# Gate maxima spread by a transfer, mLSTM products in float32r parts, first loads in small pieces, a shared last norm: one decoder layer

## The chip, the cores and the metric

The kernel runs on one core of a Trainium2 chip. The time is the device time of one execution in microseconds, as a median over runs. The engines are named as in the profile: PE is TensorE's matmul, PEld its weight load, DVE is VectorE, ACT ScalarE, POOL GpSimd, and SP the queue from which all transfers are issued. Each engine works through its own instructions in order and waits for the others by semaphores.

## The reference

One layer of a hybrid decoder, 256 tokens, model width 2048, all in float32. It has three steps, each followed by a layer norm over `alpha * x + f(x)`:

1. One input projection. Its columns go to eight attention heads of width 128 (a dilated window with a bias table), to four mLSTM heads of width 256, and to the mLSTM gates. Both groups' outputs go through one output projection.
2. Cross-attention, four heads of width 512, on 256 memory tokens.
3. A SwiGLU channel mixer, hidden width 5632.

The part that matters here is the mLSTM. With gate sums `b` and input gates `log_i`, a running maximum over time keeps the exponentials in range. Taken over all 256 tokens at once, a head is

```
u[r]      = log_i[r] - b[r],   mx[t] = max(0, u[0..t])
e[r,t]    = exp(u[r] - mx[t])  for r <= t, else 0
w[r,t]    = e[r,t] * (k[r] . q[t]) / sqrt(256)
num[t]    = sum_r w[r,t] * v[r],   den[t] = sum_r w[r,t]
h[t]      = num[t] / max(|den[t]|, exp(-(b[t] + mx[t])))
```

and `h` is normalised over its 256 columns and multiplied by the output gate. The last step of the layer is a layer norm `(z - mean) * scale * g + b` over 2048 columns, in four tiles of 512 for each half of the tokens.

## The kernel before

**Products in parts.** A float32 operand is split by `split` (L113 to L115) into a high part in float32r, by ScalarE's cast, and a low part, what is left, by VectorE's subtraction. A product is then three float32r matmuls: high by high, high by low, low by high. All large GEMMs are done so; many of them also by a seven-product scheme (`gemm_seven`). Products of operands left in plain F32 are single instructions in the program, and stand as two records each in the profile.

**Memory.** `big` gives one of 34 SBUF tiles of 128x1024 words, `slot` half of one, both reused first in, first out. PSUM has eight banks: five for GEMMs (`bank`), three for all else (`sbank`). Weights come by SP into three raw buffers of 1 MB (`RAW`), and are split into five pairs of parts (`SPLIT`).

**Order.** The program is written phase by phase: attention projections, bias table and attention, gates, mLSTM projections and heads, output projection, cross-attention, channel mixer, last norm. A planner that simulates the engines' times then orders the instructions of each engine; only one stretch (behind the second norm) has an order written by hand. So neighbouring phases overlap, and the order of all engines comes out of the planner's costs.

**Start.** A warm-up of `WARM = 2` F32 products of 512 columns on a zeroed tile (L429). Then the first projection `i0` (`gemm_features`, L387 and L388): eight steps of two k-tiles each; each step multiplies 1024 weight columns by the two tiles of x. `loader` (L181) brings x two k-tiles at a time; `weights` (L232) brings the weights, 1 MB for two steps, except the first: two halves of step 0 (L242) and step 1 by itself (L245).

**Gates.** `gates` (L510) computes `mx` as four rows (one for each head), and spreads row `h` over all 128 partitions by a product with a selecting matrix: `bc` (L551), plain F32 with four rows of contraction. VectorE forms `-mx + mask` from it (L553, L557), ScalarE the exponentials `e` (L559, L560). The selecting matrix `sel` is loaded at L794.

**mLSTM heads.** `mlstm` (L585) computes the scores (`ms`, L590), the weights `w` (L595), then for three blocks of w the products with the values (`mh`, 256 columns) and with a column of ones (`md`, one column), all in plain F32 (L603). Statistics (L608), the norm (L611 to L618), gate (L623) and transposes (L629) follow. Heads 0 and 1 stand in the program between the third value projection and `i6`, heads 2 and 3 before the keys `xk0` and `xk1`.

**End.** The last GEMM, `w2b1`, ends with the second half of the tokens; then `Norm.finish` (L719): mean and scale, four operations `(z - mean) * g` and four `z * scale + b`, all on VectorE (L726, L729), and one store for each tile (L1171).

## Time and profile before

| | us |
|---|---|
| runs | 1539.5, 1541.11, 1541.36 (median 1541.11) |
| the profiled execution's own time | 1540.81 |
| its span (first to last instruction or transfer) | 1539.0 |

| engine | busy us | share |
|---|---|---|
| PE | 1522.7 | 99% |
| DVE | 1233.4 | 80% |
| ACT | 797.0 | 52% |
| POOL | 9.3 | 1% |

The transfers move 301.37 MB, on average 196 GB/s; in the first of 40 equal slices of the span they move 303 GB/s, the most of any. The granted TensorE clock is full in all slices.

How to read the lines: a timeline line gives start and length in us, engine, line of the kernel, operation, the tiles written and read (buffer numbers left out), partitions x elements, and how many like it are merged; in brackets how long the engine sat idle before it, and what ended that. A line of waits gives who waited for whom, the sum in us, how often, and the longest. A slot keeps the name that its tile had when it was last made, so a name can be that of an earlier use.

### The profile page before, as it was taken

What the parts mean: (1) busy time and instruction counts of PE and PEld (TensorE: products, weight loads), DVE (VectorE), ACT (ScalarE), POOL (GpSimd) and SP (SyncE); (2) the same over time, 40 slices, a digit from 0 to 9 for tenths busy, and PEclk for the clock granted to TensorE, in tenths of its full rate; (3) what the DMA queues carried; (4) which work ended last, traced back from release to release, by engine and by line L of the source; (5) the groups of instructions that cost most, each with busy time, mean ns of one, the idle gap of its engine ahead of it and who ended that gap; (6) DMA issues with size and microseconds to landing.
All of it is one profiled execution on the core that took longest, in us unless ns stands there. A gap on an engine that the chain in (4) does not pass through costs nothing.

```text
span 1539.0 us, 19369 instructions
## 1 busy us (share of the span) xinstructions
PE 1522.7 (99%) x7394; PEld 1273.8 (83%) x7394; DVE 1233.4 (80%) x1663; ACT 797.0 (52%) x1054; POOL 9.3 (1%) x18
## 2 busy tenths in 40 slices
PE   9999999999999999999999999999999999999997
PEld 7888888888888878888888888887788888888885
DVE  7665788787799888657798788888788878888897
ACT  5444645554544555445557454555545455455551
POOL 0000000000000000000000000000000000000000
PEclk9999999999999999999999999999999999999999
DMA  8674445664654546445564555665455666567552
GB/s 303 208 272 165 140 172 210 232 237 160 232 191 172 205 171 221 162 165 179 177 218 165 174 182 192 218 195 200 156 215 208 200 192 194 192 205 260 197 186 109
DMA packets 83419, 301.37 MB, mean 196 GB/s; under 512 B 7213, under 2 KB 9466, under 8 KB 59774
## 3 DMA queue, kind: packets, MB, share of 16 engines
q1 hardware_dynamic: 83326, 300.14, 56.6%
q8 instruction: 58, 0.95, 0.2%
q14 instruction: 35, 0.29, 0.1%
HBM read 297.99 MB, written 4.21 MB: 196 GB/s over the span
## 4 chain that ended last, share of the span: by engine, by line
PE 95%; DVE 3%; DMA 1%; issue 0%; ACT 0%; DVEq 0%; SPq 0%; ACTq 0%
PE w2a1P L323 2%; PE w2a0P L323 2%; PE w2b0P L323 2%; PE w2b1P L323 2%; PE f10P L323 2%; PE v1P L323 2%; PE xo0P L323 2%; PE wo0P L323 2%; PE f4P L323 2%; PE f14P L323 2%; PE f6P L323 2%; PE f20P L323 2%; PE f16P L323 2%; PE f18P L323 2%; PE v0P L323 2%; PE wo1P L323 2%
## 5 line engine op out<-in xcount | busy, mean ns | idle before, releaser
L114 ACT CAST w2a1h<-w2a1w 128x1024 fp32r<-128x1024 f32 (+1 forms) x24 | 22.5, 980 | 23.3 <-PE w2a1E L323 14.5
L114 ACT CAST w2a0h<-w2a0w 128x1024 fp32r<-128x1024 f32 (+1 forms) x24 | 22.8, 980 | 17.8 <-PE w2a0E L323 10.7
L115 DVE TENSOR_TENSOR w2a0l<-w2a0w,w2a0h 128x1024 fp32r<-128x1024 f32 (+1 forms) x24 | 26.5, 1129 | 6.1 <-ACT w2a0h L114 6.1
L115 DVE TENSOR_TENSOR w2a1l<-w2a1w,w2a1h 128x1024 fp32r<-128x1024 f32 (+1 forms) x24 | 26.3, 1128 | 5.6 <-ACT w2a1h L114 5.6
L114 ACT CAST w2b0h<-w2b0w 128x1024 fp32r<-128x1024 f32 (+1 forms) x20 | 19.3, 987 | 17.3 <-PE w2b0E L323 9.8
L114 ACT CAST w2b1h<-w2b1w 128x512 fp32r<-128x512 f32 (+1 forms) x28 | 19.8, 758 | 12.9 <-PE w2b0E L323 5.4
L323 PE MATMUL w2a0P<-w2a0h,hT 128*128 128x512 f32 x80 | 26.2, 391 | 0.2 <-ACT w2a0h L114 0.2
L323 PE MATMUL w2a1P<-w2a1h,hT 128*128 128x512 f32 x80 | 25.4, 389 | 0.0
L114 ACT CAST wo1h<-wo1w 128x1024 fp32r<-128x1024 f32 (+1 forms) x16 | 15.6, 1001 | 18.9 <-PE wo1E L323 11.3
L264 PE MATMUL f0b<-f0h,x 128*128 128x512 f32 x64 | 25.4, 397 | 0.0
L114 ACT CAST f12h<-f12w 128x1024 fp32r<-128x1024 f32 (+1 forms) x16 | 15.6, 1000 | 18.7 <-PE f12E L323 9.9
L265 PE MATMUL f0b<-f0l,x 128*128 128x512 f32 x64 | 25.1, 392 | 0.1
L114 ACT CAST xv0h<-xv0w 128x1024 fp32r<-128x1024 f32 (+1 forms) x16 | 15.2, 970 | 18.5 <-PE xv0E L323 7.1
L115 DVE TENSOR_TENSOR w2b0l<-w2b0w,w2b0h 128x1024 fp32r<-128x1024 f32 (+1 forms) x20 | 22.2, 1137 | 3.0 <-ACT w2b0h L114 3.0
L115 DVE TENSOR_TENSOR v0l<-v0w,v0h 128x1024 fp32r<-128x1024 f32 (+1 forms) x16 | 18.2, 1154 | 7.8 <-ACT v0h L114 7.7
L115 DVE TENSOR_TENSOR xo0l<-xo0w,xo0h 128x1024 fp32r<-128x1024 f32 (+1 forms) x16 | 18.2, 1153 | 7.3 <-ACT xo0h L114 7.2
L114 ACT CAST v0h<-v0w 128x1024 fp32r<-128x1024 f32 (+1 forms) x16 | 15.7, 1000 | 16.0 <-PE v0E L323 9.9
L114 ACT CAST v2h<-v2w 128x1024 fp32r<-128x1024 f32 (+1 forms) x16 | 15.6, 1000 | 16.2 <-PE v2E L323 10.8
L115 DVE TENSOR_TENSOR w2b1l<-w2b1w,w2b1h 128x512 fp32r<-128x512 f32 (+1 forms) x28 | 22.7, 854 | 1.5 <-ACT w2b1h L114 1.5
L387 PE MATMUL i0b<-xT,i0h 128*128 128x512 f32 x64 | 22.6, 427 | 0.8 <-ACT i0h L114 0.8
L115 DVE TENSOR_TENSOR wo0l<-wo0w,wo0h 128x1024 fp32r<-128x1024 f32 (+1 forms) x16 | 18.2, 1153 | 6.4 <-ACT wo0h L114 6.4
L387 PE MATMUL xk1b<-mT,xk1h 128*128 128x512 f32 x64 | 23.0, 401 | 0.3 <-ACT xk1h L114 0.3
(1719 smaller groups left out, 5556.6 us busy)
## 6 DMA issues: line engine op xcount, KB each, us to landing
w2a0w<-in_w SPq DMA_DIRECT2D x12, 1024.0 KB, 4.8
w2a1w<-in_w SPq DMA_DIRECT2D x12, 1024.0 KB, 5.7
w2b0w<-in_w SPq DMA_DIRECT2D x10, 1024.0 KB, 4.9
w2b1w<-in_w SPq DMA_DIRECT2D x10, 1024.0 KB, 5.0
v0w<-in_w_v SPq DMA_DIRECT2D x8, 1024.0 KB, 5.1
v1w<-in_w_v SPq DMA_DIRECT2D x8, 1024.0 KB, 4.8
v2w<-in_w_v SPq DMA_DIRECT2D x8, 1024.0 KB, 4.8
wo0w<-in_w_out SPq DMA_DIRECT2D x8, 1024.0 KB, 4.9
```

Of the source, the lines that this page charges most:

```text
L114: SC.copy(hi, src)
L115: latest["lo"] = V.tensor_tensor(out=lo, in0=src, in1=as_f32(hi), op=ALU.subtract).ins
L264: T.matmul(banks[m][c], xh, wh[:, cs], start=n == 0, stop=False)
L265: T.matmul(banks[m][c], xh, wl[:, cs], start=False, stop=False)
L323: T.matmul(of[to], lhsT, rhs, start=to not in begun, stop=end)
L387: T.matmul(banks[f], wh[:, cs], op.both(kt), start=kt == 0, stop=end, skip_group_check=True)
```

## The change

Five edits:

- `WARM`: the second warm-up product has 256 columns in place of 512.
- `loader` and `weights`: for x and the first 1 MB of weights of `i0`, the loads are made in small pieces. x comes in single k-tiles (128 KB) for tiles 0 to 3; the weights of step 0 come in four pieces of 256 columns, those of step 1 in two of 512. Casts and subtractions follow the pieces. SP's order is: x 0, two weight pieces, x 1, two weight pieces, x 2, one weight piece, x 3, one weight piece.
- `gates`: the four rows of maxima are stored to DRAM and loaded back, repeated on all partitions, into one tile; `bc`'s products, `sel` and its load go.
- `mlstm`: the values and the weights are split into parts. The ones stand as two more columns beside the values' high part, so that the sum of the weights comes out of the same products: nine float32r products a head in place of six in F32. Each half of the tokens has its own PSUM bank, and the denominator is copied out by ScalarE.
- the last norm: for the second half of the tokens, tiles 0 and 1 are done as before, tiles 2 and 3 get `z * scale - mean * scale` from ScalarE and then a product with g and a sum with b on VectorE.

```diff
@@ -35,7 +35,7 @@
 W = 1024
 NSLOT, RAW, SPLIT = 34, 3, 5
 LAG, HEAD, POOLED, LAG2 = 6, 8, 5, 8
-WARM = 2
+WARM = (512, 256)
 
 SEVENS = (2, 4, 6, 8, 13, 15, 17)
 
@@ -178,8 +178,17 @@
         def both(self, kt):
             return self.parts[kt // 2][:, (kt % 2) * 512 : (kt % 2 + 1) * 512]
 
-    def loader(op, src):
+    def loader(op, src, fine=False):
+        def tile_alone(kt):
+            j, s = divmod(kt, 2)
+            raw = slot(f"{op.name}raw{kt}t")
+            nc.sync.dma_start(out=raw[:, :S], in_=src[j][:, s * S : (s + 1) * S])
+            hi, lo = op.views(j)
+            split(hi[:, s], lo[:, s], raw[:, :S])
+            free(raw)
 
         def load(j):
             if j not in op.parts:
@@ -188,6 +197,7 @@
                 op.put(j, raw)
                 free(raw)
 
+        load.tile_alone = tile_alone if fine else None
         return load
 
 
@@ -232,11 +242,19 @@
     def weights(src, n, name, load=None):
 
         for b in range(n // 2):
-            if load:
+            first = load is not None and b == 0
+            fine = first and load.tile_alone
+            if load and not fine:
                 load(b if n == KT else 2 * b)
-            first = load is not None and b == 0
             w = wp.tile([P, 2, W], F32, tag="w", name=f"{name}w{b}", bufs=RAW)
-            if first:
+            if fine:
+                for i in range(2):
+                    for s in range(2):
+                        load.tile_alone(2 * i + s)
+                        for c in range(2 - i):
+                            cs = slice(s * 512 + c * 256, s * 512 + (c + 1) * 256 * (1 + i))
+                            nc.sync.dma_start(out=w[:, i, cs], in_=src[b][:, i, cs])
+            elif first:
                 for c in range(2):
                     cs = slice(c * 512, (c + 1) * 512)
                     nc.sync.dma_start(out=w[:, 0, cs], in_=src[b][:, 0, cs])
@@ -251,8 +269,9 @@
                     load(at)
                 wh = wp.tile([P, W], F32R, tag="wh", name=f"{name}h{at}")
                 wl = wp.tile([P, W], F32R, tag="wl", name=f"{name}l{at}")
-                halves = (slice(0, 512), slice(512, 1024))
-                for cs in halves if first and i == 0 else (slice(0, 1024),):
+                n_cols = 256 * (1 + i) if fine else 512 if first and i == 0 else 1024
+                for c in range(0, 1024, n_cols):
+                    cs = slice(c, c + n_cols)
                     split(wh[:, cs], wl[:, cs], w[:, i, cs])
                 yield at, wh, wl
 
@@ -426,14 +445,14 @@
 
     idle, pw = slot("idle"), sbank("pw")
     G.memset(idle, 0.0)
-    for _ in range(WARM):
-        T.matmul(pw, idle[:, :P], idle, start=True, stop=True)
+    for n in WARM:
+        T.matmul(pw[:, :n], idle[:, :P], idle[:, :n], start=True, stop=True)
     free(idle)
     ones = const.tile([P, 1], F32, tag="ones", name="ones")
     V.memset(ones, 1.0)
 
     xT = Operand("xT")
-    load_x = loader(xT, A["xT"])
+    load_x = loader(xT, A["xT"], fine=True)
 
 
     def bias_table():
@@ -546,12 +565,15 @@
         V.tensor_copy(cols.rearrange("p a b -> p (a b)"), pc[:, :16])
 
         es = []
+        line = dram.tile([MH, S], F32, tag="mline", name="mline")
+        nc.sync.dma_start(out=line, in_=mx)
+        bcs = big("bcs", F32)
+        nc.sync.dma_start(out=bcs, in_=bass.AP(line.tensor, line.offset, [[0, P], [1, MH * S]]))
         for h in range(MH):
-            bc = sbank(f"bc{h}")
-            T.matmul(bc[:, :S], sel[:, h], mx, start=True, stop=True)
+            bc = bcs[:, h * S : (h + 1) * S]
             e = slot(f"me{h}")
             V.scalar_tensor_tensor(
-                out=e[:, :S].rearrange("p (m t) -> p m t", m=2), in0=bc[:, :S].rearrange("p (m t) -> p m t", m=2),
+                out=e[:, :S].rearrange("p (m t) -> p m t", m=2), in0=bc.rearrange("p (m t) -> p m t", m=2),
                 scalar=-1.0, in1=tri[:, None, :].to_broadcast([P, 2, P]), op0=ALU.mult, op1=ALU.add,
             )
             V.tensor_scalar(out=e[:, S : S + P], in0=bc[:, P:S], scalar1=-1.0, scalar2=None, op0=ALU.mult)
@@ -559,7 +581,7 @@
                 SC.activation(e[:, cs], e[:, cs], ACT.Exp, bias=cols[:, m, h : h + 1])
             SC.activation(e[:, S : S + P], e[:, S : S + P], ACT.Exp, bias=cols[:, 0, h : h + 1])
             es.append(e)
-        free(t0, t1, t2, t3, t4)
+        free(t0, t1, t2, t3, t4, bcs)
         return es, cols[:, 2:]
 
     def conv_silu(raw, ft, name):
@@ -595,19 +617,32 @@
         V.scalar_tensor_tensor(
             out=w[:, :384], in0=sc[:, :384], scalar=MD ** -0.5 / 4.0, in1=e[:, :384], op0=ALU.mult, op1=ALU.mult
         )
-        hb, dn = sbank(f"mh{h}"), sbank(f"md{h}")
-        vh = [v[r][h // 2][:, h % 2 * MD : (h % 2 + 1) * MD] for r in range(2)]
-        steps = ((0, 0, 0), (1, 0, S), (1, 1, P))
-        for n, (m, r, at) in enumerate(steps):
-            for o, x in ((hb[:, m * MD : (m + 1) * MD], vh[r]), (dn[:, m : m + 1], ones)):
-                T.matmul(o, w[:, at : at + P], x, start=n == 0, stop=n != 1, skip_group_check=True)
+        va, wa = big(f"mv{h}"), big(f"mwp{h}")
+        vh = [va[:, r * (MD + 2) : (r + 1) * (MD + 2)] for r in range(2)]
+        vl = [va[:, 2 * MD + 4 : 3 * MD + 4], wa[:, 768:]]
+        wh, wl = wa[:, :384], wa[:, 384:768]
+        for r in range(2):
+            split(vh[r][:, :MD], vl[r], v[r][h // 2][:, h % 2 * MD : (h % 2 + 1) * MD])
+            V.tensor_copy(vh[r][:, MD:], ones.to_broadcast([P, 2]))
+        split(wh, wl, w[:, :384])
+        hb = [sbank(f"mh{h}{m}") for m in range(2)]
+        for n, (m, r, at) in enumerate(((0, 0, 0), (1, 0, S), (1, 1, P))):
+            for a, x in ((wh, vh[r]), (wh, vl[r]), (wl, vh[r])):
+                cols = x.shape[-1]
+                T.matmul(
+                    hb[m][:, :cols], a[:, at : at + P], x, start=n != 2 and a is wh and cols > MD,
+                    stop=n != 1 and a is wl, skip_group_check=True,
+                )
+        free(va, wa)
         st = small.tile([P, 2, 6], F32, tag="mst", name=f"mst{h}")
         mv = small.tile([P, 2, 2], F32, tag="mmv", name=f"mmv{h}")
-        r = small.tile([P, 3, 2], F32, tag="mr", name=f"mr{h}")
+        r = small.tile([P, 4, 2], F32, tag="mr", name=f"mr{h}")
+        norm, rs, den = r[:, 0], r[:, 1], r[:, 3]
         for m in range(2):
-            V.bn_stats(out=st[:, m], in_=hb[:, m * MD : (m + 1) * MD])
+            SC.copy(den[:, m : m + 1], hb[m][:, MD : MD + 1])
+            V.bn_stats(out=st[:, m], in_=hb[m][:, :MD])
             V.bn_aggr(out=mv[:, m], in_=st[:, m])
-        den, norm, rs = dn[:, :2], r[:, 0], r[:, 1]
         V.scalar_tensor_tensor(
             out=norm, in0=den, scalar=-1.0, in1=least_norm[:, :, h], op0=ALU.mult, op1=ALU.max
         )
@@ -621,7 +656,7 @@
         for m in range(2):
             ym = y[:, m * MD : (m + 1) * MD]
             V.scalar_tensor_tensor(
-                out=ym, in0=hb[:, m * MD : (m + 1) * MD], scalar=mv[:, m, 0:1],
+                out=ym, in0=hb[m][:, :MD], scalar=mv[:, m, 0:1],
                 in1=gate[m][h // 2][:, h % 2 * MD : (h % 2 + 1) * MD], op0=ALU.subtract, op1=ALU.mult,
             )
             SC.activation(ym, ym, ACT.Copy, scale=r[:, 2, m : m + 1])
@@ -728,6 +763,21 @@
                 t = z[m][c]
                 V.scalar_tensor_tensor(out=t, in0=t, scalar=scale, in1=self.b[c], op0=ALU.mult, op1=ALU.add)
 
+        def finish_by_two(self, m):
+            mean, scale = self.scales(m)
+            shift = small.tile([P, 1], F32, tag="lsh", name=f"{self.name}sh{m}")
+            for t, g in zip(z[m][:2], self.g):
+                V.scalar_tensor_tensor(out=t, in0=t, scalar=mean, in1=g, op0=ALU.subtract, op1=ALU.mult)
+            V.scalar_tensor_tensor(out=shift, in0=mean, scalar=-1.0, in1=scale, op0=ALU.mult, op1=ALU.mult)
+            for t in z[m][2:]:
+                SC.activation(t, t, ACT.Identity, scale=scale, bias=shift)
+            for t, b in zip(z[m][:2], self.b):
+                V.scalar_tensor_tensor(out=t, in0=t, scalar=scale, in1=b, op0=ALU.mult, op1=ALU.add)
+            for t, g, b in zip(z[m][2:], self.g[2:], self.b[2:]):
+                V.tensor_tensor(out=t, in0=t, in1=g, op=ALU.mult)
+                V.tensor_tensor(out=t, in0=t, in1=b, op=ALU.add)
         def bare(self, m, scales):
 
             for t in z[m]:
@@ -789,9 +839,6 @@
     qk0 = in_features(0, load_x) + in_features(1)
     tb = bias_table()
 
-    sel_t = slot("sel")
-    sel = sel_t[:MH].rearrange("p (a b) -> p a b", a=MH)
-    nc.sync.dma_start(out=sel, in_=A["sel"])
     cw = const.tile([P, 16, 5], F32, tag="cw", name="cw")
     nc.sync.dma_start(out=cw, in_=A["conv"])
     gb = const.tile([8, 1], F32, tag="gb", name="gb")
@@ -812,7 +859,6 @@
         attention(2 * j, qk0[j], qk0[2 + j], [va[m][0] for m in range(2)], tb)
     qk1 = in_features(2) + in_features(3)
     es, least_norm = gates()
-    free(sel_t)
     for j in range(2):
         attention(4 + 2 * j, qk1[j], qk1[2 + j], [va[m][1] for m in range(2)], tb)
     free(*va[0], *va[1])
@@ -1166,7 +1212,7 @@
     banks = gemm_seven(hT, fetch(A["w2"][1][half:], "w2b1"), nkt, "w2b1", plan, into_z(1, 1.0), order, kept, True)
     for m in range(2):
         ln.add(m, 1, banks, scale=1.0)
-        ln.finish(m)
+        (ln.finish_by_two if m else ln.finish)(m)
         for c in range(4):
             nc.sync.dma_start(out=A["out"][m, c], in_=z[m][c])
 
```

## The prediction

> **What bounds the kernel now.** I read the page first (spans, busy times, chain), then TensorE's waits, then the timelines of the four places that the diff touches.
>
> ```profile
> span 1539.0 us, 19369 instructions
> PE 1522.7 (99%) x7394; PEld 1273.8 (83%) x7394; DVE 1233.4 (80%) x1663; ACT 797.0 (52%) x1054; POOL 9.3 (1%) x18
> ...
> PE 95%; DVE 3%; DMA 1%; issue 0%; ACT 0%; DVEq 0%; SPq 0%; ACTq 0%
> ```
>
> TensorE is busy 99% of the span and holds 95% of the chain that ended last. Its waits, listed longest first, are few:
>
> ```profile
> PE pw L430 <- POOL idle L428: 1.5, 1, 1.5
> ...
> PE w2a0P L323 <- ACT w2a0h L114: 0.2, 1, 0.2
> ```
>
> The eleven groups add up to 5.6 us, and all but the first are 0.8 or less. So from the first product to the last the kernel costs what TensorE takes to issue its matmuls one behind the other; 1 us of issue time taken out anywhere in between is 1 us of the end, as long as the operands still come in time. Only the start (before the first product at 6.06) and the end (behind the last at about 1528.3) follow other engines.
>
> **mLSTM's products.** One head now, on TensorE (start, length, operation; a product in plain F32 is two records):
>
> ```profile
> 298.21 0.59 PE L603 MATMUL mh<-k,v2r 128*128 128x256 f32 x2
> ...
> 300.09 0.48 PE L387 MATMUL i6b<-xT,i6h 128*128 128x512 f32 x1
> 300.41 0.28 PE L388 MATMUL i6b<-xT,i6l 128*128 128x256 f32 x1
> ...
> 300.77 0.28 PE L388 MATMUL i6b<-xT,i6l 128*128 128x256 f32 x1
> ```
>
> The six products of a head (three of 256 columns, three of one) hold TensorE from 298.21 to 300.09, and the wide i6b product behind them takes 0.32 to the next. From 300.41 to 300.77 a narrow and a wide one take 0.36, usually 0.12 and 0.235; so 0.08 more is owed to the change of type: 1.88 + 0.08 = 1.96 us. The new form has nine float32r products of 256 or 258 columns. The cross-attention scores are such products of 256 columns, each with its own weights of 128x128:
>
> ```profile
> 704.33 0.28 PE L929 MATMUL xs<-kx,qx 128*128 128x256 f32 x1
> ...
> 705.65 0.28 PE L931 MATMUL xs<-kx,qx 128*128 128x256 f32 x1
> ```
>
> Twelve of them, eleven steps in 1.32 us: 0.12 each. Two columns more are under 1% of that. Nine cost 1.08, a head saves 0.88, four heads **3.5 us**.
>
> What is added lies on other engines: per head two splits of 128x256 (values), one of 128x384 (weights), two copies of the ones, two copies of the denominator. By the nearest rows (in the two that begin with a stretch stand, in us, its length, the busy time of PE, PEld, DVE, ACT and POOL with their instructions, the granted clock, and the DMA engines' share and GB/s):
>
> ```profile
> 294.15 0.55 DVE L595 SCALAR_TENSOR_TENSOR v2r<-ms,g 128x384 f32<-128x384 f32 x1
> 300.00:318.00 18.00, 18.00 (x111) 16.02 (x110) 10.31 (x27) 6.52 (x8) 1.33 (x2) 1.00 0.65 229
> 346.00:360.00 14.00, 14.00 (x83) 12.32 (x82) 14.00 (x29) 7.36 (x9) 0.00 (x0) 1.00 0.67 213
> 352.00 1.21 DVE L115 TENSOR_TENSOR xk0l<-xk0w,xk0h 128x1024 fp32r<-128x1024 f32 x1
> 356.49 0.28 PE L388 MATMUL xk0b<-mT,xk0l 128*128 128x256 f32 x1
> ```
>
> VectorE pays 0.55 for the weights' low part (384 columns in 0.55), 2 x 0.4 for the values' and 0.2 for the ones: about 1.6 us per head. ScalarE's cast of 1024 columns takes 1.05 (a row below), so for 896 in three pieces and two tiny copies 1.5 us; it is busy 52% of the span. Between 300 and 318 VectorE is busy 10.31 of 18 us, so heads 0 and 1 are covered. Between 346 and 360 it is busy all 14 us, and the splits for heads 2 and 3 may fall there. They cost nothing while the weight parts stay ahead: the low part of xk0's sixth step is done at 353.2 and first used at 356.49, so 3.3 us are free against 2 x 1.6 = 3.2. The cover is thin; if it is gone, the excess is a wait of TensorE (rival 2). On the way from scores to products a cast and a subtraction come in between, about 1.1 us more; head 0 has 294.15 to 298.21 there, filled with other products by the planner.
>
> **Gates' maxima.** Four F32 products with four rows are removed, in two pairs:
>
> ```profile
> 161.26 1.10 PE L551 MATMUL bc<-g,tb 4*128 4x256 f32 x4
> 162.30 0.39 PE L388 MATMUL i4b<-xT,i4l 128*128 128x256 f32 x1
> ...
> 166.44 0.39 PE L387 MATMUL i4b<-xT,i4h 128*128 128x512 f32 x1
> 166.75 1.13 PE L551 MATMUL bc<-g,tb 4*128 4x256 f32 x4
> ...
> 168.03 0.39 PE L387 MATMUL i4b<-xT,i4h 128*128 128x512 f32 x1
> ```
>
> First pair: 161.26 to 162.30, 1.04. Second: 166.44 to 168.03 is 1.59, in which a wide i4b product has its 0.235 and a narrow one its 0.12: 1.24. Together **2.3 us** off TensorE. In their place stand a store of 4 KB to DRAM and a load of 512 KB that repeats it on all partitions, both in SP's queue, the second waiting for the first, and the weight loads of i5 and v1 behind it. The nearest round trip is the bias table's:
>
> ```profile
> SPq L453 <- DMA line<-i1r: 3.7, 1, 3.7
> 164.00 1.05 ACT L114 CAST i5h<-i5w 128x1024 fp32r<-128x1024 f32 x1 [1.38 <-PE i4b L387]
> 177.51 0.40 PE L387 MATMUL i5b<-xT,i5h 128*128 128x512 f32 x1
> ```
>
> 3.7 us for a store to be readable, about as much again for the load. Behind SP the next weights wait, behind VectorE's reading of the maxima the low parts of i5. But ScalarE made i5's first part at 164.00 and TensorE used it at 177.51: a stop of up to 10 us on either queue is covered, and the exponentials themselves are first read at 294.15. I cost it at nothing; without that cover it would be the 7 us of the round trip, less what is stocked. The `sel` load of 8 KB goes.
>
> **First loads.** On SP (issues), ScalarE (casts) and TensorE:
>
> ```profile
> 0.74 0.39 SPq L187 DMA_DIRECT2D xTraw<-in_xT  x1
> ...
> 3.54 0.55 SPq L247 DMA_DIRECT2D i0w<-in_w_qk  x1
> ...
> 5.55 0.50 SPq L247 DMA_DIRECT2D i0w<-in_w_qk  x1
> ```
>
> ```profile
> 3.40 0.62 ACT L114 CAST xT<-xTraw 128x512 fp32r<-128x512 f32 x1 [1.39 <-DMA xTraw<-in_xT]
> 5.39 1.28 ACT L114 CAST i0h<-i0w 128x512 fp32r<-128x512 f32 x2 [1.37 <-DMA i0w<-in_w_qk]
> ...
> 11.73 2.00 ACT L114 CAST i0h<-i0w 128x1024 fp32r<-128x1024 f32 x2 [1.53 <-DMA i0w<-in_w_qk]
> ```
>
> ```profile
> 1.46 3.78 PE L430 MATMUL pw<-idle 128*128 128x512 f32 x4 [1.46 <-POOL idle L428]
> 6.06 2.07 PE L387 MATMUL i0b<-xT,i0h 128*128 128x512 f32 x4 [0.82 <-ACT i0h L114]
> ...
> 13.94 1.08 PE L387 MATMUL i0b<-xT,i0h 128*128 128x512 f32 x4
> ```
>
> An issue takes SP 0.4 to 0.5, so six follow the first by 3.54. The tenth (5.55) went out only when the second's data had landed (cast at 5.39), and so it goes on: I read it as no more than eight loads under way at once. The seventh, at 3.54, is the 1 MB for steps 2 and 3, cast at 11.73 to 12.73 and used from 13.94.
>
> After the change ten pieces of 128 to 256 KB come in place of five loads. The first products need two pieces of 128 KB in place of two of 256 KB (cast at 3.40 and 5.39): I put the second at 4.2, between these, so products start at about 4.6, 1.4 us sooner; the shortened warm-up (three quarters of 3.78, to 4.3) is then over. Steps 0 and 1 hold TensorE for 13.94 - 6.06 = 7.9 us now, at most as long then, to 12.5. But the 1 MB load becomes SP's twelfth issue, at 0.74 + 11 x 0.45 = 5.7 in place of 3.54. The bytes ahead of it are the same 1.8 MB. If their pace is kept, step 2's weights are cast at 12.73 as now and the start gains at most 13.94 - 12.73 = 1.2; if the load slips by the whole 2.2 us of its issue, step 2 is ready at 14.9 and the start loses 1.0. Steps 4 and later have more room. Since the bytes ahead are equal and SP issues a 128 KB piece per 0.45 (290 GB/s), I am nearer to the first: a gain of **0.5 us**, ends +1.2 and -1.0.
>
> **Last norm.** VectorE now:
>
> ```profile
> 1530.53 1.40 DVE L726 SCALAR_TENSOR_TENSOR z<-z,l2mv,f20h 128x512 f32<-128x512 f32 x2
> ...
> 1534.50 1.41 DVE L729 SCALAR_TENSOR_TENSOR z<-z,l2r,l2b 128x512 f32<-128x512 f32 x2
> 1530.76 0.91 POOL L716 TENSOR_TENSOR l2r<-l2r,mhalf 128x1 f32<-128x1 f32 x1 [9.13 <-DVE l2r L715]
> 907.12 0.68 DVE L745 TENSOR_TENSOR z<-z,l1b 128x512 f32<-128x512 f32 x1
> 907.72 0.68 DVE L691 TENSOR_TENSOR f2ru<-f2ru,f2P 128x512 f32<-128x512 f32 x1
> ```
>
> Eight operations at a step of 0.66 (six steps in 3.97) end at 1535.9. After: two of these (to 1531.85, when POOL's scale of 1531.67 is there), the shift (0.2), two more (to 1533.37), and four plain ones, whose step is 0.60: 1535.85. ScalarE's two, 0.8 each at most, are done by 1533.7, before VectorE asks for the second. Nothing is gained: eight full-width operations stay on VectorE. Bounds: 0.1 less, 0.4 more if the dependent pairs don't overlap. I take **0**.
>
> **Sum.** 3.5 + 2.3 + 0.5 + 0 = 6.3 us off the profiled execution's own 1540.81 (1.8 outside its span of 1539.0): **1534.5**. That execution lies 0.3 under the median of the runs shown, well inside their spread.
>
> **Rivals.** 1: *the small pieces starve the start.* Eight under way are then 1 to 1.25 MB, where the seventh alone was 1 MB. Pieces of this size stand in the bias table's loads (median us to landing; then a stretch of them with DMA share and GB/s):
>
> ```profile
> tb<-rows SPq DMA_DIRECT2D x6, 128.0 KB, 3.1
> 84.00:85.00 1.00, 1.00 0.84 178
> ```
>
> 3.1 us for 128 KB, and 178 GB/s moved while these and pieces of 64 KB follow each other. At that pace the 1.05 MB in eight pieces take 5.9 us, not the 3.6 that SP's issues allow; step 2 comes 2.3 late, a loss of 1.1 in place of 0.5 gained: 1536.1. The Trainium skill's "DMA: Bandwidth & Descriptors", section Bandwidth, speaks against the change in the same way: it asks for DMAs of 1 MiB and gives 138 GB/s for 64 KB, 341 for 1 MB; the bias table's 178 fits between.
>
> 2: *the longer way from scores to products shows.* If the planner finds nothing to fill the 1.1 us of each head, or VectorE's full stretch passes them on, TensorE waits 4 x 1.1 = 4.4: 1538.9. For it: heads 2 and 3 stand close (VectorE full). Against: the 4 us that head 0 has, and only 5.6 us of waits in all with every split done this way.
>
> 3: *slower: 258 columns do not run at float32r's rate.* No product of that width is in the trace. Three wide and three one-column products of F32 take 1.88 us, so a wide one is between 0.31 and 0.63; at the middle, 0.47, 36 of them add 36 x 0.35 = 12.6: 1547.1. It decides from 0.12 + 6.3/36 = 0.295 us a product. Against: 256 columns take 0.12 and 512 take 0.235, one rate for both.
>
> 4: *the gain is lost in the new order.* The order of all engines is planned anew with other costs; were the waits of 5.6 us to double, 1540.1.
>
> **Chances.** Forecast 0.60, rival 1 0.15, rival 2 0.13, rival 3 0.04, rival 4 0.08. A measurement of this kernel tells about 0.2% (3.1 us) from no change: below 1538.0 against the median is faster. Forecast and rival 1 give 0.75 faster, rivals 2 and 4 0.20 about the same (with a little of 4 beyond), rival 3 and that remainder 0.05 slower. Range: downwards the start's full 1.2 and the runs' spread below their median (1.6) give 1532.2; upwards rival 2 and some of the spread, 1539.5.
>
> **What would show it.** mLSTM: nine records of a head 0.12 apart, no wait of TensorE on the split parts; a wait named after them of over 0.5 speaks for rival 2, steps near 0.4 for 3. Gates: no product at that place and no stop of i5's or v1's products within 30 us. Start: the first product near 4.6 and step 2 at 13.4 or before; later than 13.94 is rival 1. End: VectorE still about 7.6 us behind the last product. A time over 1538 with all of these right would put the cause into the new order.

## The result and the profile after

| | before | changed |
|---|---|---|
| median of the runs, us | 1540.86 | 1561.15 |
| lowest to highest | 1539.5 to 1541.36 | 1556.44 to 1562.78 |
| profiled execution: span | 1539.0 | 1560.0 |

The changed kernel takes 1.0128 times as long, with an interval of 1.0105 to 1.0152. It is 20.3 us slower; 1534.5 had been forecast. From the page after, and from TensorE's waits, longest first:

```profile
span 1560.0 us, 19400 instructions
PE 1527.1 (98%) x7374; PEld 1275.6 (82%) x7374; DVE 1240.5 (80%) x1689; ACT 804.9 (52%) x1081; POOL 9.8 (1%) x18
...
PE 90%; DVE 5%; DMA 3%; issue 1%; ACT 1%; SPq 0%; DVEq 0%; ACTq 0%
```

```profile
PE xk0b L406 <- DVE mT L115: 5.9, 3, 2.6
PE i0b L406 <- ACT i0h L114: 3.8, 3, 1.9
PE pt L516 <- DVE xTr L512: 2.5, 1, 2.5
PE pt L516 <- DVE g L512: 2.4, 1, 2.4
```

TensorE has 20 instructions fewer, yet is busy 4.4 us longer, and it stands idle 32.9 us (1560.0 - 1527.1) in place of 16.3. Three waits are new or much longer: for the memory tokens' parts (`xk0b` on `mT`), for the first weights (`i0b`, 0.8 before), and, twice, of attention's transposes (`pt`) for their exponentials. None is a wait for the maxima's transfer, and on mLSTM's split parts stands one of 0.3 us (`mh` on `mwp`).

Where the time goes is read from the last product of a GEMM, in the views of single tiles (its start; the differences are those of the ends). A line gives operation, count, shortest, median and longest in ns, and the first and the last start in us. Before:

```profile
L388 PE MATMUL i5b<-xT,i5l x64: 274/280/365, 177.7 to 203.0; 128*128 128x256 f32 x64
L388 PE MATMUL xk1b<-mT,xk1l x64: 277/281/385, 363.4 to 395.9; 128*128 128x256 f32 x64
L323 PE MATMUL w2b1E<-w2b1l,hT x14: 389/389/389, 1483.2 to 1528.1; 128*128 128x512 f32 x14
```

After:

```profile
L407 PE MATMUL i0b<-xT,i0l x64: 274/280/583, 5.8 to 33.4; 128*128 128x256 f32 x64
L407 PE MATMUL i5b<-xT,i5l x64: 274/281/415, 183.6 to 217.1; 128*128 128x256 f32 x64
L407 PE MATMUL xk1b<-mT,xk1l x64: 274/280/388, 369.5 to 417.9; 128*128 128x256 f32 x64
L342 PE MATMUL w2b1E<-w2b1l,hT x14: 389/389/389, 1504.4 to 1549.3; 128*128 128x512 f32 x14
```

The last i5 product comes 14.1 us late, xk1's 22.0, the very last 21.2. So behind the keys, from 418 us to the end, nothing is lost any more. Of single tiles read the same way, the first features (`i0`) end 2.8 us late, `i2` 3.4, `i5` 14.1, `i7` 11.3, `xk1` 22.0. That makes three places: the start (+2.8), the attention heads among i3 to i5 (about +11), the keys (about +11), with some gain between them. The profiled execution is the slowest of the four, so these sizes are a little above those of the median.

### The profile page after: what moved, and what is told of

It is laid out like the page before. It is cut to its first block, busy times and chain, and to the rows that moved or that the text cites. A ratio compares the mean times of both kernels' runs of the same rounds, so it can differ in the third digit from the quotient of the medians.

```text
span 1560.0 us, 19400 instructions
## 1 busy us (share of the span) xinstructions
PE 1527.1 (98%) x7374; PEld 1275.6 (82%) x7374; DVE 1240.5 (80%) x1689; ACT 804.9 (52%) x1081; POOL 9.8 (1%) x18
## 4 chain that ended last, share of the span: by engine, by line
PE 90%; DVE 5%; DMA 3%; issue 1%; ACT 1%; SPq 0%; DVEq 0%; ACTq 0%
PE w2a1P L342 2%; PE w2a0P L342 2%; PE w2b0P L342 2%; PE w2b1P L342 2%; PE f10P L342 2%; PE xo0P L342 1%; PE v1P L342 1%; PE f14P L342 1%; PE f6P L342 1%; PE f4P L342 1%; PE f20P L342 1%; PE f18P L342 1%; PE wo0P L342 1%; PE f16P L342 1%; PE f2P L342 1%; PE xo1P L342 1%
## 5 line engine op out<-in xcount | busy, mean ns | idle before, releaser
L406 PE MATMUL xk0b<-mT,xk0h 128*128 128x512 f32 x64 | 25.2, 432 | 6.7 <-DVE mT L115 5.9
L114 ACT CAST w2b0h<-w2b0w 128x1024 fp32r<-128x1024 f32 (+1 forms) x20 | 19.2, 988 | 17.0 <-PE w2b0E L342 10.1
L114 ACT CAST wo1h<-wo1w 128x1024 fp32r<-128x1024 f32 (+1 forms) x16 | 15.6, 1000 | 18.9 <-PE wo1E L342 11.3
L114 ACT CAST f12h<-f12w 128x1024 fp32r<-128x1024 f32 (+1 forms) x16 | 15.6, 1000 | 18.7 <-PE f12E L342 11.3
L114 ACT CAST v0h<-v0w 128x1024 fp32r<-128x1024 f32 (+1 forms) x16 | 15.7, 999 | 16.6 <-PE v0E L342 10.1
L114 ACT CAST wo0h<-wo0w 128x1024 fp32r<-128x1024 f32 (+1 forms) x16 | 15.7, 999 | 15.1 <-PE wo0E L342 8.1
```

The source lines that it names most:

```text
L114: SC.copy(hi, src)
L406: T.matmul(banks[f], wh[:, cs], op.both(kt), start=kt == 0, stop=end, skip_group_check=True)
```

## The experiments

All kernels but e13 are the kernel before with parts of the change. All compute the whole layer. Times are medians; the ratio is to runs of the kernel before on the same chip.

| | us | before | ratio, 95% interval |
|---|---|---|---|
| e1 gates alone | 1550.54 | 1540.41 | 1.0068 [1.0053, 1.0083] |
| e2 mLSTM alone | 1545.59 | 1540.41 | 1.0032 [1.002, 1.0045] |
| e3 start alone | 1543.32 | 1540.41 | 1.0019 [1.0009, 1.0028] |
| e4 norm alone | 1540.23 | 1540.41 | 1.0 [0.9991, 1.0009] |
| e5 gates, half tile kept | 1539.28 | 1540.22 | 0.9994 [0.9984, 1.0003] |
| e6 mLSTM, tiles to the front | 1546.79 | 1540.22 | 1.0039 [1.0024, 1.0054] |
| e7 e5 + e6 + norm | 1545.59 | 1540.22 | 1.0032 [1.0021, 1.0042] |
| e8 start, step 0 only | 1541.39 | 1540.22 | 1.0005 [0.9996, 1.0015] |
| e9 mLSTM, heads 0 and 1 | 1540.37 | 1540.87 | 0.9997 [0.9988, 1.0006] |
| e10 e5 + e9 + norm | 1538.9 | 1540.87 | 0.9992 [0.9983, 1.0001] |
| e11 e6, filler held back | 1540.26 | 1540.77 | 0.9999 [0.999, 1.0008] |
| e12 e5 + e11 + norm | 1538.71 | 1540.77 | 0.9989 [0.998, 0.9999] |
| e13 whole change, repaired | 1541.62 | 1540.38 | 1.0005 [0.9996, 1.0015] |
| e14 warm-up alone | 1540.31 | 1540.38 | 1.0 [0.999, 1.0009] |

### One part at a time (e1 to e4)

e1, the gates' edit as in the diff shown ahead, nothing else:

```diff
-            bc = sbank(f"bc{h}")
-            T.matmul(bc[:, :S], sel[:, h], mx, start=True, stop=True)
+        nc.sync.dma_start(out=bcs, in_=bass.AP(line.tensor, line.offset, [[0, P], [1, MH * S]]))
...
-    sel_t = slot("sel")
...
-    free(sel_t)
```

> The kernel before with the gates' edit alone (maxima spread through DRAM, sel gone). Theory A (the newly planned order costs it, the edit itself is free): TensorE's order differs from before from i2b on to the end of the key/value features, the products of i3 that stood between the chunk scores and the transposes of their exponentials fall from 57 to 3, waits of TensorE for VectorE's exponentials of about 2.5 us appear near 140 and 200 us, the clock drops there, and the last i5 product ends 9 to 11 us later than before; from there at most 3 us more; time 1548 to 1552. Rival B (the edit is worth its 2.3 us, and the loss comes from mLSTM's added VectorE and ScalarE work or from the sum of the edits): 1538 to 1540, no wait above 1 us. Rival C (the DRAM round trip holds up SP's queue and VectorE): a wait of TensorE for weights or parts issued behind the round trip, between 165 and 200 us, of 3 us or more.

e2, mLSTM's edit alone:

```diff
-        hb, dn = sbank(f"mh{h}"), sbank(f"md{h}")
+        va, wa = big(f"mv{h}"), big(f"mwp{h}")
...
+        hb = [sbank(f"mh{h}{m}") for m in range(2)]
...
+        free(va, wa)
```

> The kernel before with mLSTM's edit alone. Theory A (replanned order): as before up to the first mLSTM head (i5's end within 0.3 us of before), products at 0.12 us, then the keys' products of xk0 end 5 to 10 us late because they wait for the memory tokens' parts, and the clock falls there; time 1543 to 1549. Rival B (the edit pays its 3.5 us when it stands alone, and only the start and the gates cost): 1537 to 1538. Rival D (VectorE's added work in its full stretch is what shows, 1.1 us a head): 1540 to 1542, with waits for split parts of 1 us or less.

e3, the start alone:

```diff
-WARM = 2
+WARM = (512, 256)
...
-    load_x = loader(xT, A["xT"])
+    load_x = loader(xT, A["xT"], fine=True)
```

> The kernel before with the first loads in small pieces and the shorter warm-up alone. Theory A: first product near 4.1 us, but a wait of 1.5 us and more for the later pieces and for step 2's weights, the clock back at half between them, and the first features end 2.5 to 3 us later than before, constant from there: 1543 to 1544. Rival B (the start recovers once the order behind it is the old one): 1540 to 1541.

e4, the last norm alone:

```diff
-        ln.finish(m)
+        (ln.finish_by_two if m else ln.finish)(m)
```

> The kernel before with the last norm shared with ScalarE alone, its order of work on TensorE unchanged. Theory A: the time between the last product and the end of the span 10.5 in place of 10.7 us, nothing else: 1540 to 1541, not to be told from before. Rival B (ScalarE's part or the plain operations of VectorE hold up the stores): 1542 or more, the tail above 11.5 us.

Measured: +10.1, +5.2, +2.9 and -0.2 us. They sum to 18.0 of the 20.3. The 2.3 us left are no more than the intervals of the four allow, so no effect of the edits on one another is shown. The ends of single tiles say where. With the gates alone i5 ends 9.1 us late and xk1 10.9; with mLSTM alone i5 ends 0.3 late, xk0 12.8 (5 to 10 were expected) and xk1 7.4; with the start alone the first features end 2.1 late. So theory A holds in each place, if not in each size, and rivals B and C fall: the edits cost where the order or the loads changed, not where the new work stands.

How a gates' edit reaches back to attention, which stands ahead of it in the program, is in e1's timeline (start, length, engine, operation; in brackets the idle time before it and what ended it):

```profile
134.22 0.39 PE L480 MATMUL sc<-i0r 128*128 128x128 f32 x2
...
137.60 0.30 PE L497 MATMUL pt<-ident,xTr 128*128 128x128 f32 x1 [2.53 <-DVE xTr L493]
...
137.94 0.37 ACT L402 COPY xTr<-i2b 128x256 f32<-128x256 f32 x1 [1.26 <-PE pt L497]
...
138.58 0.38 ACT L402 COPY xTr<-i2b 128x256 f32<-128x256 f32 x1
```

And the same work in the kernel before:

```profile
127.19 0.38 ACT L402 COPY xTd<-i2b 128x256 f32<-128x256 f32 x1 [2.07 <-PE pt L497]
127.83 0.39 ACT L402 COPY xTd<-i2b 128x256 f32<-128x256 f32 x1
...
132.40 0.38 PE L480 MATMUL sc<-i0r 128*128 128x128 f32 x2
...
142.50 0.27 PE L497 MATMUL pt<-ident,apT 128*128 128x128 f32 x1
```

i2's PSUM banks are copied out into half tiles. Before, the last copy was at 127.83, behind the transposes of the head before. In e1 the last two wait until the transposes of a head have read their exponentials: the copy's target and the transposes' source are one tile (`xTr`). The banks are held until then. i3 needs four of the five GEMM banks, so I read it that most of i3's products cannot stand between that head's scores and transposes any more. The transposes come 3.4 us behind the last score (134.22 to 137.60) instead of 10.1, as soon as the exponentials are ready, and TensorE waits 2.53 us of it. Without `sel`'s half tile the ring of free tiles, first in first out, gave i2's copies other tiles than before; that is all that connects the two.

### Giving the tiles back their places (e5 to e7)

e5 keeps the half tile, empty, and all else of the gates' edit:

```diff
+    sel_t = slot("sel")
...
     es, least_norm = gates()
+    free(sel_t)
```

> The gates' edit alone, but the half tile that the selecting matrix had is still taken and given back at the old places, empty (no load of it, no product). The transfer, VectorE's reading of it and the missing products are those of the edit alone. By the planned order the 57 products of i3 between scores and transposes are back. Theory A2 (the loss of the edit alone came from the other tiles that i2's features and attention's exponentials got once the half tile was gone, not from the transfer): no wait of TensorE for exponentials above 0.8 us, i5 ends about 2.3 us earlier than before, time 1538.1 (1537.5 to 1539). Rival C (the round trip costs it): i5 still ends 7 us or more late, 1548 and more. Rival E (both: the order gives back the 9 us, the round trip costs what the products gave): 1540 to 1541.

1539.28, 11.3 us less than e1 for an empty half tile. No wait on `pt` is left, and i5 ends 2.4 us earlier than before: the 2.3 us of the four products. Nothing but the empty half tile differs between e1 and e5, so the tile, and the order that comes with it, is shown to be the cause. The transfer itself, in e5's timeline:

```profile
159.20 0.28 SPq L550 DMA_DIRECT2D mline<-g  x1
162.01 0.35 SPq L552 DMA_DIRECT2D bcs<-mline  x1
...
166.08 0.43 DVE L556 SCALAR_TENSOR_TENSOR g<-bcs,tri 128x256 f32<-128x256 f32 x1 [2.67 <-DMA bcs<-mline]
```

From the store's issue to VectorE's first reading pass 6.9 us; VectorE waits 2.67 of them, TensorE nothing at that place. Rival C, with its wait of 3 us or more, falls for good. By the end of v1 the lead has shrunk to 1.5 us, 0.6 of it in a wait for a low part at 217.80 (`v1P` on `v1l`). Kernels without the gates' edit have no such wait on `v1l`; whether it comes from VectorE's 2.67 us, 50 us earlier, or from TensorE being sooner is not shown. So theory A2 holds on the cause. Its size is 0.9 us by the medians where 2.3 were expected, with an interval from 2.5 gained to 0.5 lost, which does not decide between 2.3 and nothing.

In mLSTM alone (e2), SP's waits in the keys' stretch and the end of one of them:

```profile
SPq L187 <- PE mh L611: 11.1, 2, 10.2
```

```profile
373.18 0.28 PE L611 MATMUL mh<-mv,mwp 128*128 128x258 f32 x1
...
373.49 0.33 SPq L187 DMA_DIRECT2D mTraw<-in_memT  x1
...
376.23 0.62 ACT L114 CAST mT<-mTraw 128x512 fp32r<-128x512 f32 x1 [2.57 <-DMA mTraw<-in_memT]
...
377.63 0.80 PE L387 MATMUL xk0b<-mT,xk0h 128*128 128x512 f32 x1 [2.94 <-DVE mT L115]
```

The last load of the memory tokens goes out at 373.49, as soon as head 3's last product has let go of its parts' tile; before, it went out at 344.21. The keys then wait for it. e6 gives the parts' tiles to the next user instead of the ring's end:

```diff
-        free(va, wa)
+        for t in (wa, va):
+            free_slots.insert(0, held.pop(id(t))[0])
```

> mLSTM's edit alone, but the two tiles of a head's parts go back to the front of the ring of free tiles, so that the next user takes them and all later tiles fall where they fell before; in the edit alone the last two memory-token loads got tiles that heads 2 and 3 still held. Theory A2 (that is what cost it): the memory-token loads are all issued by 346 us as before, no wait of TensorE for their parts, mLSTM's nine products at 0.12 us, time 1540.4 - 3.5 = 1536.9 (1536 to 1538). Rival D (VectorE's and ScalarE's added work costs it): waits for split parts around 345 to 365 us remain, 1540 to 1542.

1546.79: no better. Half of the theory held. The last of these loads goes out at 341.66, no wait on `mT` is left, and xk0 ends 1.6 us earlier than before, where it ended 12.8 late in e2. But xk1 still ends 6.5 late. e6's timeline at head 2 shows a wait that nobody had on the list:

```profile
368.90 0.28 PE L611 MATMUL mh<-mv,mwp 128*128 128x258 f32 x1
...
373.54 0.69 POOL L632 TENSOR_TENSOR mr<-mr,mhalf 128x2 f32<-128x2 f32 x1 [37.92 <-DVE mr L631]
...
374.27 0.91 ACT L641 ACTIVATE v1r<-v1r,mr 128x256 f32<-128x256 f32 x2 [3.99 <-POOL mr L632]
...
374.83 0.69 PE L643 MATMUL mpt<-ident,v1r 128*128 128x128 f32 x2 [3.25 <-ACT v1r L641]
```

From the head's last product over statistics, norm, POOL's power and the scaling to the transposes it takes 5.9 us, and there is nearly no product in between: 16 key products that stood there before now stand in the middle of the head's nine (four from 365.12, the other five from 368.42). Theory A2 was wrong on this part. Rival D named neither the place nor the size, though a wait of 1.1 us for split weights (`mh` on `mwp`, ahead of head 3's products) is of its kind.

e7 puts e5, e6 and the norm together:

> Both of these together with the shared last norm, without the edit of the start. If the savings add: 1540.4 - 2.3 - 3.5 - 0.1 = 1534.5 (1533.5 to 1536). If they were one and the same time of TensorE or the order falls badly again: 1537 to 1541.

1545.59, outside both expectations: the same 3.2 us wait on `mpt` as in e6 spoils it, with the gates' gain of about 1 us on top.

### mLSTM once more (e9 to e12)

e9 has the new products for heads 0 and 1 only:

```diff
+        if h < 2:
             va, wa = big(f"mv{h}"), big(f"mwp{h}")
...
+        else:
+            hw, dn = sbank(f"mh{h}"), sbank(f"md{h}")
```

> mLSTM's float32r products for heads 0 and 1 alone, heads 2 and 3 in plain F32 as before; the two tiles of the parts go back to the front of the ring. Theory F (heads 2 and 3 carry the loss: between them the planner has only some 20 key products, and the way from the scores over the parts, the products, the norm to the transposes is too long to be filled; a wait there costs twice because the clock falls): no wait of TensorE on mpt or mh above 1 us, the last product of xk1 1.5 to 2 us earlier than before, time 1540.3 - 2 x 0.88 = 1538.5 (1537.8 to 1539.8). Rival G (any head in the new form costs): 1542 or more, with waits near 300 us.

1540.37, against 1546.79 with all four heads (e6), and the clock stays up: theory F is right on where the large loss sits. But 1.8 us were expected and 0.5 came, within what can be told from no change. In the profiled execution 1.1 us are gained between the ends of i5 and i7, and a wait of 1.0 us for xk1's weights (0.3 before) takes most of it back. Their cast goes out at 370.06 in both kernels, when xk0's last products have let go of a part. The products themselves are as cheap as forecast. Head 0 in e9:

```profile
299.16 0.64 PE L612 MATMUL mh<-mv,mwp 128*128 128x258 f32 x4
299.63 0.39 PE L387 MATMUL i6b<-xT,i6h 128*128 128x512 f32 x1
...
300.68 0.53 PE L612 MATMUL mh<-mv,mwp 128*128 128x258 f32 x3
301.04 0.28 PE L612 MATMUL mh<-mwp 128*128 128x256 f32 x1
301.16 0.28 PE L612 MATMUL mh<-mv,mwp 128*128 128x258 f32 x1
301.28 0.39 PE L387 MATMUL i6b<-xT,i6h 128*128 128x512 f32 x1
```

Four in 0.47 and five in 0.60 us: 1.07 for nine.

e10 joins e9, e5 and the norm:

> Heads 0 and 1 in float32r parts, the gates' edit with the half tile kept, the shared last norm, the start of before. Theory F with the gates' measured gain: 1540.3 - 0.9 to 2.3 - 1.8 = 1536.2 to 1537.6. If the savings do not add because another wait appears: 1538.5 to 1540.5.

1538.9: the savings do not add in full. That wait of 1.0 us is there again, and one of 0.9 on v1's low parts.

e11 has all four heads in the new form again, with e6's tiles, and holds 16 key products behind head 2's last product:

```diff
+LATE = {'xk0': (7, 'mh2')}
...
+                with tc.issue_after(latest[LATE[name][1]]) if name in LATE and n == LATE[name][0] else nullcontext():
                     T.matmul(banks[f], wh[:, cs], op.both(kt), start=kt == 0, stop=end, skip_group_check=True)
```

> mLSTM's edit for all heads, the parts' tiles back to the front of the ring, and the 16 key products of xk0's last step held behind head 2's last product, so that they stand between it and head 2's transposes as in the kernel before (in the run without that they stood ahead of head 2's last five products). Theory O (the order took the filler away): the wait on mpt of 3.2 us falls to 0.5 or less, the clock stays up, xk1 ends 2 us or more earlier than before, time 1537 to 1538.5. Theory L (the way itself is too long: 16 products last 2.9 us, and the way from the last product over the statistics and the norm to the transposes took 5.6): a wait of 1.5 to 3 us stays at head 2 or at head 3, the clock falls there, 1540 to 1545.

In its timeline the wait ahead of the transposes is down to a sixth:

```profile
367.14 0.28 PE L613 MATMUL mh<-mv,mwp 128*128 128x258 f32 x1
...
371.22 0.50 PE L389 MATMUL xk1b<-mT,xk1h 128*128 128x512 f32 x1 [1.02 <-ACT xk1h L115]
...
372.23 0.44 PE L645 MATMUL mpt<-ident,v1r 128*128 128x128 f32 x2 [0.50 <-ACT v1r L643]
```

1540.26, 6.5 us less than e6, and the granted clock stays at 1.00. So theory O is right on what the order took. Yet of the 3.5 us saved on the products only 0.5 reach the end (by the interval from 1.5 gained to 1.2 lost), and theory L is right on that, though not on the clock. The way from product to transposes is still 5.1 us, the 16 products fill about 3, and 1.02 + 0.50 remain here and 0.5 more ahead of head 3's products: 2.0 where before 0.3 were. The 1.02 us come with the filler: the cast of those xk1 weights waits for the last of the 16 products and starts at 370.12. The other 1.3 us have no row of their own.

e12 adds the gates with the half tile and the norm:

> The same with the gates' edit (half tile kept) and the shared last norm, the start of before. Theory O: 1534.5 to 1537. Theory L: 1538.5 to 1543.

1538.71, 2.1 us below before, ratio 0.9989 [0.998, 0.9999]: the lowest median of the study, not to be told from e10 and e5. The time lies in theory L's range, by the same waits as in e11.

### The start (e8, e14) and the whole (e13)

e3's start, and the moved bytes. First product and step 2 in e3:

```profile
4.63 2.07 PE L406 MATMUL i0b<-xT,i0h 128*128 128x512 f32 x4 [0.25 <-ACT i0h L114]
5.91 0.43 SPq L265 DMA_DIRECT2D i0w<-in_w_qk  x1
...
13.98 2.00 ACT L114 CAST i0h<-i0w 128x1024 fp32r<-128x1024 f32 x2 [1.85 <-DMA i0w<-in_w_qk]
15.08 1.19 PE L406 MATMUL i0b<-xT,i0h 128*128 128x512 f32 x4 [1.89 <-ACT i0h L114]
```

Two stretches before and in e3 (length, busy time of PE, PEld, DVE, ACT, POOL, the granted clock, the DMA engines' share, GB/s). Before:

```profile
6.00:8.00 2.00, 1.94 (x5) 1.55 (x6) 1.94 (x3) 1.25 (x3) 0.00 (x0) 1.00 1.03 393
8.00:10.00 2.00, 2.00 (x8) 1.78 (x7) 0.39 (x2) 1.36 (x2) 0.00 (x0) 1.00 1.04 434
```

In e3:

```profile
6.00:8.00 2.00, 2.00 (x10) 1.68 (x9) 1.08 (x3) 1.05 (x3) 0.00 (x0) 1.00 0.86 215
8.00:10.00 2.00, 1.81 (x10) 1.43 (x9) 1.09 (x3) 1.03 (x2) 0.00 (x0) 1.00 0.94 293
```

The first product starts at 4.63, 1.4 us earlier. But from 6 to 10 us the transfers move 215 and 293 GB/s where before they moved 393 and 434, though the DMA engines are nearly as busy (0.86 and 0.94 against 1.03 and 1.04): small pieces are still under way then, and before the 1 MB was. Over these 4 us that is 0.64 MB less, 1.5 us at the old pace. The 1 MB is also issued 2.4 us later (5.91 against 3.54) and cast 2.3 later (13.98 against 11.73), so this run does not tell the slower pace from the later issue. Step 2's products follow at 15.08, before at 13.94. The first features end 2.1 us late; the further 1.0 us behind step 2 was not followed. The execution profiled is the fastest of e3's ten.

e8 has small pieces for step 0 alone:

```diff
+                for s in range(2):
+                    load.tile_alone(s)
+                    for c in range(2):
+                        cs = slice(s * 512 + c * 256, s * 512 + (c + 1) * 256)
+                        nc.sync.dma_start(out=w[:, 0, cs], in_=src[b][:, 0, cs])
+                load(1)
+                nc.sync.dma_start(out=w[:, 1], in_=src[b][:, 1])
```

> The edit of the start alone, cut to step 0: two x tiles and four pieces of its weights come in small loads, step 1 and all behind it in the loads of before, the warm-up is the short one. The 1 MB for steps 2 and 3 is then SP's ninth load in place of the twelfth (seventh before). Theory (the loss of the start comes from the 1 MB that is issued late): its issue near 4.4 us, its cast near 12.7 to 13, first product near 4.5, the first features end between 0.5 us early and 0.7 late against the kernel before; time 1540 to 1541. Rival (small pieces themselves are slow, or the short warm-up leaves the clock at half): the first features end 2 us late as with the whole edit, 1542 to 1543.5.

1541.39 lies between the two. The profiled execution speaks for the rival: the first product starts at 3.96, step 1's weights are cast at 10.56 (8.64 before), TensorE waits 2.85 us for them, the clock is at half for 3.4 us from 13.3 on, and the first features end 2.6 late. So it is not only the 1 MB for steps 2 and 3 that comes late: the load behind the small pieces does, whichever it is. Its issue is late too (4.02 against 2.59), so pace and issue are not told apart here either.

e14 has the shorter warm-up alone, on the loads of before:

```diff
-    for _ in range(WARM):
-        T.matmul(pw, idle[:, :P], idle, start=True, stop=True)
+    for n in WARM:
+        T.matmul(pw[:, :n], idle[:, :P], idle[:, :n], start=True, stop=True)
```

> The kernel before with the shorter warm-up alone, its loads as they were. If the loads in small pieces make the whole loss at the start: first product near 6.06 us and the first features end within 0.5 us of before, 1540 to 1541.5. If the warm-up has a part (1.7 us without a product before the first real one let the clock fall): products of steps 0 and 1 at half clock, first features 1 us late or more, 1542.

1540.31, the time of before. Its profiled execution, the slowest of its ten, shows a wait of 1.78 us, then the clock at half for 3.4 us from 11.6 on, and first features 1.4 late. The medians do not confirm it; by their interval a loss of up to 1.4 us is left open. The profiled executions speak for a part of the warm-up: of the five with the shorter one, four (the changed kernel, e8, e13 and e14) have 3.4 us at half clock within their first 20 us, and of the eleven with the old one none has.

e13 is the changed kernel whole with the three repairs of order (e5's half tile, e6's tiles, e11's filler):

> The changed kernel whole, with its start, and only these repairs: the selecting matrix's half tile kept empty, the parts' tiles back to the front of the ring, xk0's last 16 products behind head 2's. If the three places (start, attention, keys) are all of the 20 us: the run with the start of before measured 1538.7, the start alone costs 2.9, so 1541 to 1542.5. If something of the loss lies elsewhere or the edits act on one another: 1545 or more.

1541.62, within the first expectation. It has all the edits of the changed kernel and takes 19.5 us less (1561.15). Against e12 the start's 2.9 are there. So the three places are all of the loss, as far as the medians tell.

## Why the prediction was wrong, step by step

**The step that failed** is the price of the new order. The prediction gave it to rival 4, with a chance of 0.08 and a doubling of the 5.6 us of waits (1540.1). It was 19.5 us (e13), of the 26.7 between the forecast and the measured 1561.15; the rest lies in the terms below. That step took the order as a matter of costs. What moved it were tiles: removing a half tile, and taking two more tiles a head, changed who gets which tile from the ring, and so which work must end before which. The description of the kernel names the ring (first in, first out), and the prediction never asked what each edit does to it. Nor did it price a wait beyond its own length, though several also cost clock (below). Its last sentence, that a time over 1538 with all else right puts the cause into the new order, pointed the right way, although not all else was right.

**mLSTM, 3.5 us.** Products right: 1.07 a head against 1.08, so rival 3 falls. Costing the added work at nothing was wrong. The cover looked at was VectorE's between 346 and 360; the one that was missing was TensorE's between head 2's products and its transposes, where the kernel before already had only some 20 products. Rival 2 comes nearest, with 4.4 us for the four heads, but it named the way from the scores to the products, where e11 has 0.5 us of wait. With the order repaired 3.0 of the 3.5 are lost (e11, by the medians), 1.7 of them in waits near that place.

**Gates, 2.3 us.** Right on TensorE (2.4 by the end of i5) and on the transfer: 6.9 us long against the 7 named, with no wait of TensorE at that place. At the end 0.9 remain by the medians (e5), too few to tell from 2.3 or from nothing; in the trace a wait for a low part in v1 takes 0.6.

**First loads, +0.5.** The first product is about where it was put (4.63 in e3, 4.11 in the changed kernel, against 4.6), step 2 is not (15.08 against 13.4). The term that failed is "if their pace is kept": it was not, 215 against 393 GB/s. The prediction's own other end, a load that slips by the whole of its issue, put step 2 at 14.9, and rival 1, a slower pace, put it 1.1 later than before; both fit, and no run separates them. Neither covers what is lost behind step 2: e3's medians show 2.9, its profiled execution 2.1 at the end of the first features. That a wait in the start can cost clock stood in no term. The Trainium skill's "DMA: Bandwidth & Descriptors", section Bandwidth, asks for DMAs of 1 MiB or more; 215 against 393 GB/s points the same way.

**Last norm, 0.** Right: -0.2 (e4).

**Bound.** TensorE stays busy in 98% of the span (90% of the chain that ended last, before 95%), and the time behind 420 us is the same to 0.8 us. The condition "as long as the operands still come in time" was written down and then checked only for the new work, not for the old work that moved.

## What to carry to other kernels

Where a planner orders the work and tiles are recycled first in, first out, an edit that takes or drops a tile is an edit of everything behind it: list who waits for whose tile before and after, and keep an empty tile in its place if need be. A product taken off a busy engine is worth its time only if the next thing that engine must wait for does not move further behind than that. And small first loads start the first product sooner while the bytes of the next steps come later.

## What the runs showed of the hardware

A wait of TensorE can cost more than its length. In e1 it waits 1.46 us at 376, for the memory tokens (columns as above):

```profile
376.00:377.00 1.00, 0.00 (x0) 0.00 (x0) 1.00 (x5) 0.52 (x1) 0.00 (x0) 1.00 0.28 115
377.00:378.00 1.00, 0.67 (x3) 0.63 (x4) 1.00 (x5) 0.00 (x0) 0.00 (x0) 0.90 0.00 0
378.00:379.00 1.00, 1.00 (x4) 0.81 (x4) 1.00 (x5) 0.00 (x0) 0.00 (x0) 0.50 0.00 0
380.00:381.00 1.00, 1.00 (x5) 0.81 (x5) 0.00 (x0) 0.85 (x2) 0.11 (x1) 0.50 0.00 0
381.00:382.00 1.00, 1.00 (x7) 0.92 (x7) 0.00 (x0) 0.19 (x2) 0.00 (x0) 0.89 0.00 0
```

The granted clock falls to 0.50 within 377 to 378 and is back within 381 to 382. A mean of 0.90 is 0.2 us at half and one of 0.89 is 0.22, so with the 3 us between them it is 3.4 us at half, and the work in them takes 1.7 us more. With the wait that is 3.2 of the 3.5 us that e1 loses in the keys, where its order is nearly that of before. In e6 the clock stays at half for 10.2 us. In the changed kernel four stretches have a clock below 1.00 ahead of the last product:

```profile
14.00:21.00 7.00, 6.04 (x25) 4.95 (x26) 6.51 (x9) 6.47 (x9) 0.00 (x0) 0.76 1.03 404
141.00:147.00 6.00, 6.00 (x38) 4.91 (x39) 0.51 (x2) 1.44 (x4) 0.00 (x0) 0.72 0.00 0
199.00:208.00 9.00, 7.76 (x28) 6.59 (x29) 6.39 (x17) 3.97 (x10) 0.00 (x0) 0.62 0.00 0
390.00:399.00 9.00, 6.93 (x25) 5.75 (x26) 5.42 (x15) 4.66 (x10) 1.12 (x1) 0.62 0.29 115
```

Reckoned in the same way they are 3.4, 3.4, 6.8 and 6.8 us at half, about 10 us more. This closes the account of the profiled execution: 16.6 us more idle, about 10 more for the clock, less the 5.8 of products saved, makes about the 21.0 by which the span grew, and it is why TensorE is busy longer with fewer instructions.

No length of wait decides it alone: e3 waits 1.89 us ahead of 15.08, the changed kernel 1.52 and 1.73 us ahead of 376.44 and 381.26, and the clock stays at 1.00 behind them. The Trainium skill's "TensorE: Matmul & The Clock Gate", section "Why this matters for your kernels", asks for no gaps above about 3 us between bursts; by e1 half of that is enough. The 3.4 us fit the window that the same page gives in "What's actually happening".
